# A hybrid decoder layer on one core: residual rows kept whole for the second norm, and a fixed matmul order at the mixer's end

## The chip, the cores and the metric

The kernel runs on one core of one Trainium2 chip. The metric is the device time of one execution in microseconds (us). Its engines work side by side, each through its own list of instructions in order: TensorE (PE: matmuls, and transposes as matmuls with an identity), VectorE (DVE), ScalarE (ACT) and GpSimd (POOL); SyncE (SP) starts most of the DMAs. Semaphores hold an instruction back until what it reads is there and what it overwrites is no longer needed.

## The reference

One layer on 1024 tokens of width 1024, all in float32:

```python
h = rms_norm(x, norm_mix)
xa, ga, q, f, v, g, m_a, m_b = split(h @ w_in)            # eight projections, 1024 wide each
xa  = causal_depthwise_conv(xa, conv_w, conv_b)
y_a = rg_lru(xa, ...) * gelu(ga)                          # linear recurrence along the tokens
o   = rms_norm(hgrn2_chunkwise(silu(q), k(f), log_f, v), hg_norm)   # gated attention in chunks of 32
y   = sigmoid(m_a) * y_a + sigmoid(m_b) * (o * silu(g))
x   = x + y @ w_out
h   = rms_norm(x, norm_mlp)
x   = x + square(relu(h @ w_up)) @ w_down                 # 1024 -> 4096 -> 1024
return rms_norm(x, norm_final)
```

## The kernel before

The tokens are two halves of 512 (`c` = 0, 1). The mixer walks through each half in four pairs of heads (`p` = 0 to 3): `project` multiplies the normed half by a group of weight columns (the tiles `pj_xa`, `pj_q`, `pj_f`, `pj_g`, `pj_mb`, `pj_ga`, `pj_ma`), `project_v` does so for two pairs at once (`pv`), `conv` and `rg_lru` make one branch (`xc`, then the products `pr` and `pi`, the tiles `rw`, `rr`, `ri`, `h`), `hgrn` the other (`qa`, `kb`, `qb`, `kk`, `qn` on VectorE; scores `sc` and the transposed keys `pk` on TensorE), and `gates` merges them (`on`, `gel`). Every product is split into three matmuls (`mm3`): both operands are kept as a high and a low part, made from the float32 tile by `split` (L81), a cast on ScalarE (`wH`) and a subtraction on VectorE (`wL`). So each weight tile that comes in (`raw`) costs both engines some time.

After the first half, `out_proj` multiplies the gated result by `w_out` in two passes of 512 columns (`hf` = 0, 1; four row tiles of 128 tokens each, product tiles `po`). Between the passes `first_norm` norms and transposes the second half's rows (`norm_rows`, `transposed`; rows `x`, result `xn`). `res0` loads the residual's piece into `xs` (128x512, two buffers), VectorE adds `po` to it (L739), and `done0` stores the sum to `x2d` in HBM. The rows come back whole in `early_norm` (tile `x2a`), are normed into `xna_h` and stored again, to be fetched at the mixer's end. `early_sums` adds blocks of the first weights of the MLP (tiles `qa0`, `qb0`, `qa1`, `qb1`, of the input `mlp_in`) and stores the sums. Both are written in the loop over the pairs of the second half, and their instructions lie around pair 0.

The MLP multiplies by Strassen's scheme with seven products: per group of hidden columns ("quad") the products `uX`, `uY`, `uZ` come from parts of the normed rows (`h2B11`, `h2B21`, `h2t1`, `h2n2`, `h2T3`, `h2B22`, `h2T4`) and of the weights (`wA...` for a block itself, `ws...` for sums), the first accumulating into PSUM banks from which ScalarE copies intermediate values `e`. `wA` are splits of the quad's raw tiles `q`; the raw sums `s` come back from HBM.

At the mixer's end the second half's output projection (`po`) is interleaved with the transposes of the first half's rows (`early_half`), and the last row tiles follow: `stats` squares and norms (`x2s` to `xn_h`, L888 to L892), `turned` transposes (`xT_h`, L868), `late_ops` makes the Strassen combinations. Up to there the program order of TensorE's matmuls is fixed (`pe_order[0]`, `keep_in_program_order`); from row tiles 6 and 7 (`tt` = 2, 3) on the scheduler sets it by priorities. `hidden(q, step)` issues one product and empties its bank; steps 0 and 3 of quads 0 and 1 (`uX` and `uZ`) come first, then the loop over the quads. x's rows of tiles 6 and 7 are stored to HBM as `x_6` and `x_7`.

Of the kernel before, what the change touches and what calls it, by code (L numbers as in the profile page):

```python
# [42 lines left out]
def trunk(ctx: ExitStack, tc: tile.TileContext, x, wts, mlp, pv, gains, mask_f, mask_u, out):  # L43
# [100 lines left out]

    def norm_rows(xt, xn, gain, name):
        r = const.tile([P, 1], F32, tag="rstd", name=f"rstd_{name}", bufs=4)
        keep(A.activation(xn, xt, AF.Square, scale=D**-0.5, accum_out=r))
# [1 line left out]
        keep(G.tensor_tensor(out=r, in0=r, in1=mhalf[:, 0:1], op=ALU.pow))
        keep(V.scalar_tensor_tensor(xn, xt, r[:, 0:1], gain, op0=ALU.mult, op1=ALU.mult))  # L150
# [93 lines left out]
    X_TAGS = ("g1", "g2", "on", "xc")  # L244

    def first_norm():
        dst = a2_set(a2h, "hT1")
        xts = [tile_x(f"x{4 + tt}") for tt in range(4)]
        for tt in range(4):
            nc.sync.dma_start(xts[tt], x[(4 + tt) * P : (5 + tt) * P, :])  # L250
        xns = {}

        def rows(tt):
            xns[tt] = mt("f" if tt % 2 == 0 else "tmp", f"xn1{tt}", (P, D))
            norm_rows(xts[tt], xns[tt], gain0[0], f"x1{tt}")

        rows(0)
# [639 lines left out]
    def late_rows(tt, tag, pin):  # L897
        turned(xns[tt], tag, f"h{4 + tt}", pin)

    def late_ops(o, tt):  # L900
        b11, b21, b12, b22 = parts(tt)
        if o == "t1":
            V.tensor_tensor(out=b11, in0=b11, in1=b12, op=ALU.subtract)
            op_split(b11, "t1", tt)
        elif o == "n2":
            V.tensor_tensor(out=b12, in0=b22, in1=b12, op=ALU.subtract)
            op_split(b22, "B22", tt)
            V.scalar_tensor_tensor(b22, b11, -1.0, b22, op0=ALU.mult, op1=ALU.subtract)
            op_split(b22, "n2", tt)
        elif o == "T3":  # L910
            op_split(b12, "T3", tt)
# [156 lines left out]

    e_first = ust.tile([P, 2, T], F32, tag="u2", name="e0_01", bufs=3)

    def hidden(q, step):
        bk, wo, ho = PLAN[step]
        first = (q, bk) not in bank_of
        if first:
            bank_of[q, bk] = bank(BANK[bk], f"u{bk}{q}")
# [2 lines left out]
        o, b = bank_of[q, bk], b_of[q]
        wh, wl = ops_w[q][wo]
        hh, hl = hop[ho]  # L1080
        for k in range(4):
            cols = slice(k * P, (k + 1) * P)
            mm3(o, wh[:, cols], wl[:, cols], hh[:, k, :], hl[:, k, :], first and k == 0, k == 3, not first)
# [28 lines left out]

    for q in (0, 1):
        load_quad(q)
        work[q] = quad_steps(q, (w1p, wp))
        with tc.high_priority(200):
            work[q]["a"]()
            if q == 0:
                work[0]["d"]()
            else:  # L1120
                work[1]["one"]("A12", w1p.tile([P, 2, 512], F32R, tag="w1", name="wA12_1", bufs=3))
        if q == 0:
            work[0]["sums"]()
# [206 lines left out]
```

## Time and profile before

| | |
|---|---|
| median of three runs | 1577.17 us (1572.2 to 1577.4) |
| the profiled execution | 1579.71 us, its span 1577.5 us |
| TensorE busy | 1552.7 us (98%) |
| TensorE weight loads | 1280.6 us (81%) |
| VectorE busy | 1197.6 us (76%) |
| ScalarE busy | 787.2 us (50%) |
| mean granted TensorE clock | 0.998 |

The span runs from the first to the last instruction. Rows of the waits name the waiting instruction, then what released it, then us in total, times, longest. Rows of the timeline have the start in us, the duration, engine, line, operation, tiles, shapes, and in brackets the idle time of the engine before them with what ended it; `x4` behind a row says that it stands for four such instructions. Rows of the chain have start, length and what.

### The profile page before, as it was taken

To read this page: it belongs to the slowest core of one execution; us is meant where nothing else is said; L and a number is where in the kernel's file an instruction comes from. 1 tells how busy PE (TensorE), PEld (TensorE's weight loads), DVE (VectorE), ACT (ScalarE), POOL (GpSimd) and SP (SyncE) were. 2 spreads that over 40 slices of the span, in tenths; PEclk is the share of its full clock that TensorE was granted. 3 is DMA by queue.
4 is the path that set the end of the run, shared out by engine and by line. 5 is a ranking of instruction groups with operands and counts; after the bars stand their busy time and mean duration, and the time that the engine had idled before them with its cause. 6 is when DMAs were issued, how large, how long until landed. Compare 5 with 4: busy or idle time off the path is not lost.

```text
span 1577.5 us, 22878 instructions
## 1 busy us (share of the span) xinstructions
PE 1552.7 (98%) x9002; PEld 1280.6 (81%) x9002; DVE 1197.6 (76%) x1746; ACT 787.2 (50%) x1255; POOL 76.8 (5%) x105
## 2 busy tenths in 40 slices
PE   9999999999999999999999999999999999999998
PEld 7788888888887778888888887888888878888886
DVE  5886954968763877955969788877788888888875
ACT  5644544556442644544545576776777632211115
POOL 1010000010100010000000000000000000000002
PEclk9999999999999999999999999999999999999999
DMA  6222222222245532222322454666666665666652
GB/s 231 94 81 94 91 71 93 95 74 94 88 160 200 199 110 94 95 81 83 105 80 88 146 208 151 268 252 252 248 249 252 222 265 226 246 251 254 254 211 107
DMA packets 61019, 254.88 MB, mean 162 GB/s; under 512 B 7152, under 2 KB 7280, under 8 KB 50160
## 3 DMA queue, kind: packets, MB, share of 16 engines
q1 hardware_dynamic: 59328, 248.18, 43.3%
q10 hardware_dynamic: 1584, 5.25, 1.0%
q8 instruction: 70, 1.15, 0.3%
q14 instruction: 37, 0.30, 0.1%
HBM read 189.44 MB, written 63.96 MB: 161 GB/s over the span
## 4 chain that ended last, share of the span: by engine, by line
PE 86%; DVE 9%; issue 2%; DMA 2%; ACT 1%; POOL 0%; DVEq 0%; SPq 0%; ACTq 0%; POOLq 0%
PE dX L122 10%; PE uX L122 9%; PE pj_ma L122 6%; PE pj_xa L122 6%; PE dY L122 5%; PE pj_ga L122 5%; PE pj_q L122 5%; PE pj_f L122 5%; PE uY L122 5%; PE po L122 4%; PE pj_g L122 4%; PE pj_mb L122 4%; PE pv L122 4%; PE dZ L122 2%; PE uZ L122 2%
## 5 line engine op out<-in xcount | busy, mean ns | idle before, releaser
L83 DVE TENSOR_TENSOR wL<-raw,wH 128x1024 fp32r<-128x1024 f32 x153 | 187.1, 1224 | 120.2 <-ACT wH L82 119.7
L82 ACT CAST wH<-raw 128x1024 fp32r<-128x1024 f32 x155 | 162.8, 1051 | 161.1 <-issue 34.9
L1240 DVE TENSOR_TENSOR acc<-acc,dX 128x512 f32<-128x512 f32 x128 | 86.8, 683 | 30.3 <-PE dX L122 29.7
L82 ACT CAST wA<-q 128x512 fp32r<-128x512 f32 x34 | 20.8, 621 | 131.1 <-DMA q<-mlp_in 102.6
L1240 DVE TENSOR_TENSOR acc<-acc,dY 128x512 f32<-128x512 f32 x64 | 43.4, 685 | 17.7 <-PE dY L122 15.5
L429 DVE RECIPROCAL rr<-rr 128x512 f32<-128x512 f32 x16 | 53.5, 3346 | 0.0
L1091 ACT ACTIVATE b<-b 128x512 f32<-128x512 f32 x48 | 30.2, 630 | 35.3 <-DVE b L1090 35.3
L1201 POOL TENSOR_TENSOR acc<-acc,gain 128x512 f32<-128x512 f32 x8 | 10.4, 1299 | 605.5 <-ACT junk L1198 605.2
L122 PE MATMUL uX<-h2B11H,wA 128*128 128x512 f32 x128 | 39.8, 391 | 0.0
L666 ACT ACTIVATE on<-po 128x128 f32<-128x128 f32 x64 | 16.9, 280 | 37.4 <-PE po L662 37.3
L540 POOL TENSOR_SCALAR seg<-seg 128x128 f32<-128x128 f32 (+1 forms) x16 | 19.2, 1202 | 290.5 <-DVE seg L468 290.5
L395 DVE SCALAR_TENSOR_TENSOR xc<-xp,pvt,xc 128x512 f32<-128x512 f32 x48 | 33.1, 747 | 0.0
L1092 ACT ACTIVATE b<-b 128x512 f32<-128x512 f32 x48 | 30.0, 630 | 1.1
L670 DVE TENSOR_SCALAR hssq<-hssq 128x8 f32<-128x8 f32 x8 | 1.4, 172 | 36.1 <-ACT on L666 36.1
L122 PEld LDWEIGHTS uX<-h2B11H,wA 128*128 128x128 f32 x128 | 23.9, 188 | 4.9
L122 PE MATMUL pj_ga<-hT0L,wH 128*128 128x512 f32 x64 | 26.9, 420 | 0.0
L122 PE MATMUL pj_ga<-hT1L,wH 128*128 128x512 f32 x64 | 26.5, 414 | 0.0
L122 PE MATMUL pv<-wL,hT1H 128*128 128x512 f32 x64 | 25.2, 394 | 0.8 <-DVE xs L739 0.8
L122 PE MATMUL pj_mb<-hT1L,wH 128*128 128x512 f32 x64 | 25.4, 396 | 0.0
L122 PE MATMUL pj_mb<-hT0L,wH 128*128 128x512 f32 x64 | 25.4, 396 | 0.0
L122 PE MATMUL pj_ga<-hT0H,wL 128*128 128x512 f32 x64 | 25.4, 396 | 0.0
L122 PE MATMUL uX<-h2B11L,wA 128*128 128x512 f32 x64 | 25.0, 391 | 0.3 <-ACT wA L82 0.3
(1641 smaller groups left out, 5136.7 us busy)
## 6 DMA issues: line engine op xcount, KB each, us to landing
raw<-wts_in SPq DMA_DIRECT2D x157, 512.0 KB, 3.4
q<-mlp_in SPq DMA_DIRECT2D x64, 512.0 KB, 3.6
x<-x_in SPq DMA_DIRECT2D x8, 512.0 KB, 5.9
acc<-x ACTq DMA_DIRECT2D x8, 512.0 KB, 6.2
y_out<-acc SPq DMA_DIRECT2D x16, 256.0 KB, 2.2
xs<-x_in SPq DMA_DIRECT2D x8, 256.0 KB, 4.5
x<-xs SPq DMA_DIRECT2D x8, 256.0 KB, 2.1
x2a<-x SPq DMA_DIRECT2D x4, 512.0 KB, 5.1
```

Source lines behind the costliest of these rows:

```text
L82: keep(A.copy(h, src))
L83: keep(engine.tensor_tensor(out=lo, in0=src, in1=h.bitcast(F32), op=ALU.subtract))
L122: ins = PE.matmul(o, a, b, start=begin, stop=end, **how)
L395: V.scalar_tensor_tensor(xc[:, s, :], xp[:, j : j + T], pvt[:, PV_CW + 8 * j + u : PV_CW + 8 * j + u + 1], xc[:, s, :], op0=ALU.mult, op1= ...
L429: V.reciprocal(rec, rec)
L540: G.tensor_scalar(after[:, :, 2], t4[:, :, 3], 1.0, 0.0, op0=ALU.mult, op1=ALU.add)
L666: A.activation(on[:, 4 * s + n, :], po[:, n * P : (n + 1) * P], AF.Square, accum_out=ssq[:, 4 * s + n : 4 * s + n + 1])
L670: V.tensor_scalar(ssq, ssq, 1.0 / P, EPS, op0=ALU.mult, op1=ALU.add)
L1091: A.activation(b[:, at, :], b[:, at, :], AF.Relu, scale=-1.0 if at == 2 else 1.0)
L1092: A.activation(b[:, at, :], b[:, at, :], AF.Square)
L1201: G.tensor_tensor(out=x2[t][:, cols], in0=x2[t][:, cols], in1=gain2[:, cols], op=ALU.mult)
L1240: V.tensor_tensor(out=dst, in0=dst, in1=banks[bk, pr], op=op)
```

## The change

1. Residual rows of the first half. `rows0` holds four whole rows tiles `xr0` to `xr3` (128x1024) in buffers that the mixer uses at other times (`X_TAGS`), loaded once in front of the first half's output projection. `res0` returns a slice of them; the sum is made in place, stored to `x2d`, and `early_norm` norms it from there. The loads `xs` and `x2a` are gone, and all four `early_norm` are called ahead of pair 0 of the second half.
2. The first norm of row tile 4 (`first_row(0)`) is called in `gates` of pair 3 of the first half, behind `on`, and its place in VectorE's order is fixed.
3. At the mixer's end the order of TensorE stays fixed through the products of steps 3 and 0 of quads 0 and 1 and the transposes of row tiles 6 and 7. The product (`products`) is issued apart from the emptying of its bank (`emptied`). The first weight splits and `e` get tiles in a pool that is free there (`w_first`, `e_first`), and the late combinations come in another order (`late_ops`).
4. The stores `x_6`, `x_7` go in front of the second sum load of quad 1.

```diff
-        keep(V.tensor_scalar(r, r, EPS, None, op0=ALU.add))
+        ins = keep(V.tensor_scalar(r, r, EPS, None, op0=ALU.add))
+        if pinned:
+            tc.keep_in_program_order(ins)
...
+    def first_row(tt):
+        xt = tile_x(f"x{4 + tt}")
+        nc.sync.dma_start(xt, x[(4 + tt) * P : (5 + tt) * P, :])
+        first_rows[tt] = mt("f" if tt % 2 == 0 else "tmp", f"xn1{tt}", (P, D))
+        norm_rows(xt, first_rows[tt], gain0[0], f"x1{tt}", tt == 0)
...
         on = on[0]
+        if c == 0 and p == NPAIR - 1:
+            first_row(0)
...
     def res0(tt, hf):
-        xs = xt_pool.tile([P, 512], F32, tag="xs", name=f"xs{tt}{hf}", bufs=2)
-        nc.sync.dma_start(xs, x[tt * P : (tt + 1) * P, hf * 512 : (hf + 1) * 512])
-        return xs
+        return rows0[tt][:, hf * 512 : (hf + 1) * 512]
...
     def early_norm(tt):
-        xs, xn = tile_x(f"x2a{tt}"), tile_x(f"xna_h{tt}")
-        nc.sync.dma_start(xs, x2d[tt])
-        norm_rows(xs, xn, gain1, f"h{tt}")
+        xn = tile_x(f"xna_h{tt}")
+        norm_rows(rows0[tt], xn, gain1, f"h{tt}")
...
+            for tt in range(4):
+                rows0.append(mt(X_TAGS[tt], f"xr{tt}", (P, D)))
+                nc.sync.dma_start(rows0[tt], x[tt * P : (tt + 1) * P, :])
             out_proj(0, ys, res0, done0, first_norm)
             gain1 = gain_tile(1)
+            for tt in range(4):
+                early_norm(tt)
...
-    pe_order[0] = False
-    for tt in (2, 3):
-        nc.sync.dma_start(x2d[4 + tt], x2s[tt])
-        late_rows(tt, "sc", False)
-    for o in ("t1", "n2", "T3", "T4"):
-        for tt in (2, 3):
-            late_ops(o, tt)
...
+    w_first = [a2y.tile([P, 4, 512], F32R, tag="a2", name=f"wA1{j}", bufs=4) for j in range(2)]
+    load_quad(0)
+    work[0] = quad_steps(0, (None, wp))
+    with tc.high_priority(200):
+        work[0]["one"]("A11", w_first[0][:, 0:2, :])
+        work[0]["d"]()
+    work[0]["sums"]()
+    products(0, 3)
+    nc.sync.dma_start(x2d[6], x2s[2])
+    late_rows(2, "sc", True)
+    products(0, 0)
+    load_quad(1)
...
+    products(1, 0, last_rows)
+    products(1, 3)
+    pe_order[0] = False
...
-    for q in (0, 1):
-        load_quad(q)
...
-        hidden(q, 0)
-        hidden(q, 3)
...
+    for step in (0, 3):
+        for q in (0, 1):
+            with tc.high_priority(200):
+                emptied(q, step)
```

`last_rows` is called inside `products(1, 0)` and, behind the second of its four groups, stores row tile 7 and transposes it.

On VectorE, in pair 3 of the first half, ahead of `kb` in the `hgrn` chain, the kernel before has

```order
L83 TENSOR_TENSOR wL_3486<-raw_3483,wH_3485 128x1024
L468 TENSOR_TENSOR seg_3375<-seg_3375 128x16
L148 TENSOR_SCALAR rstd_x_4079<-rstd_x_4079 128x1
L468 TENSOR_TENSOR seg_3375<-seg_3375 128x8
L150 SCALAR_TENSOR_TENSOR xn_4078<-x_4070,rstd_x_4079,gain_143 128x1024
L468 TENSOR_TENSOR kb_3374<-kb_3374,seg_3375 128x128x6
L468 TENSOR_TENSOR dd_3373<-sc_03_3531,mf 128x256
```

and the changed kernel, at the same place,

```order
L692 TENSOR_TENSOR g_3446<-g_3446,pj_g_1_3385 128x512
L84 TENSOR_TENSOR wL_3486<-raw_3483,wH_3485 128x1024
L469 TENSOR_TENSOR seg_3375<-seg_3375 128x16
L469 TENSOR_TENSOR seg_3375<-seg_3375 128x8
L469 TENSOR_TENSOR kb_3374<-kb_3374,seg_3375 128x128x6
L469 TENSOR_TENSOR dd_3373<-sc_03_3531,mf 128x256
```

so `rstd_x` and `xn`, the norm of row tile 4, have left the chain.

On VectorE, from the convolution of pair 0 of the second half (`xc`) to `q`, the kernel before has the sums of the first quad in between (L767 to L770):

```order
L385 COPY xp_5351<-xcar 128x3
L767 TENSOR_TENSOR qb_6135<-qa_6134,qb_6135 128x512
L83 TENSOR_TENSOR wL_4558<-raw_4555,wH_4557 128x1024
L83 TENSOR_TENSOR xcL_4520<-xc_4504,xcH_4519 128x1024
L385 COPY xp_5358<-xcar 128x3
L768 TENSOR_TENSOR qa_6134<-qa_6134 128x512
L769 TENSOR_TENSOR qa_6134<-qb_6135,qa_6134 128x512
L770 TENSOR_TENSOR qb_6135<-qa_6134,qb_6135 128x512
L449 TENSOR_TENSOR q_4585<-sq_4586,pj_q_0_4523 128x256x2
```

In the changed kernel the last norm and both quads' sums stand ahead of the convolution:

```order
L153 SCALAR_TENSOR_TENSOR xna_h_4313<-xr_3940,rstd_h_4314,gain_4290 128x1024
L84 TENSOR_TENSOR wL_4392<-raw_4389,wH_4391 128x1024
L84 TENSOR_TENSOR wL_4422<-raw_4419,wH_4421 128x1024
L769 TENSOR_TENSOR qb_6128<-qa_6127,qb_6128 128x512
L770 TENSOR_TENSOR qa_6127<-qa_6127 128x512
L771 TENSOR_TENSOR qa_6127<-qb_6128,qa_6127 128x512
L772 TENSOR_TENSOR qb_6128<-qa_6127,qb_6128 128x512
L84 TENSOR_TENSOR wL_4458<-raw_4455,wH_4457 128x1024
L84 TENSOR_TENSOR wL_4488<-raw_4485,wH_4487 128x1024
L769 TENSOR_TENSOR qb_6140<-qa_6139,qb_6140 128x512
L770 TENSOR_TENSOR qa_6139<-qa_6139 128x512
```

Four rows later follows the first `xc`; the second quad's sums, and the norm `xna_h` that stood ahead of `kk` in pair 0, have left the recurrence and the `hgrn` chain.

On TensorE at the mixer's end, behind the last `po`, the kernel before has (`uX_8577` is quad 0's, and row tile 7's transposes lie in quad 1's `uX` in the same way)

```order
L122 MATMUL uZ_8592<-h2B21H,wA120L 128x512
L122 MATMUL uZ_8592<-h2B21L,wA120H 128x512
L122 MATMUL uX_8577<-h2B11L,wA_8566 128x512
L868 MATMUL xT_h_0_8441<-ident,xn_h_8250 128x128 x4
L868 MATMUL xT_h_1_8447<-ident,xn_h_8250 128x128 x4
L122 MATMUL uX_8577<-h2B11H,wA_8566 128x512 x2
L122 MATMUL uX_8577<-h2B11L,wA_8566 128x512
```

with four `uZ` matmuls ahead of this `uX` and eight behind it; the changed kernel has all twelve `uZ` first:

```order
L123 MATMUL uZ_8440<-h2B21L,wA120H 128x512
L123 MATMUL uZ_8440<-h2B21H,wA120H 128x512
L123 MATMUL uZ_8440<-h2B21H,wA120L 128x512
L872 MATMUL xT_h_0_8454<-ident,xn_h_8234 128x128 x4
L872 MATMUL xT_h_1_8460<-ident,xn_h_8234 128x128 x4
L123 MATMUL uX_8466<-h2B11L,wA_8424 128x512
L123 MATMUL uX_8466<-h2B11H,wA_8424 128x512 x2
```

Row tile 6's transposes thus moved behind eight more matmuls, and nothing behind them may pass.

More of the change, by code (lines that the diff above doesn't have):

```diff
@@ L79, in keep @@
             tc.keep_in_program_order(ins)
+        return ins
     def split(src, h, lo, engine=V):
@@ L142, in gain_tile, with norm_rows @@
         return g
-    def norm_rows(xt, xn, gain, name):
+    def norm_rows(xt, xn, gain, name, pinned=False):
         r = const.tile([P, 1], F32, tag="rstd", name=f"rstd_{name}", bufs=4)
         keep(A.activation(xn, xt, AF.Square, scale=D**-0.5, accum_out=r))
-        keep(V.tensor_scalar(r, r, EPS, None, op0=ALU.add))
+        ins = keep(V.tensor_scalar(r, r, EPS, None, op0=ALU.add))
+        if pinned:
+            tc.keep_in_program_order(ins)
         keep(G.tensor_tensor(out=r, in0=r, in1=mhalf[:, 0:1], op=ALU.pow))
@@ L244, in trunk @@
     X_TAGS = ("g1", "g2", "on", "xc")
+    first_rows = {}
+    def first_row(tt):
[3 more added lines that the diff above has]
+        norm_rows(xt, first_rows[tt], gain0[0], f"x1{tt}", tt == 0)
     def first_norm():
         dst = a2_set(a2h, "hT1")
[L248 to L257, printed above, removed]
         for tt in range(4):
             if tt < 3:
-                rows(tt + 1)
-            transposed(xns[tt], dst, tt, f"x1{tt}")
+                first_row(tt + 1)
+            transposed(first_rows[tt], dst, tt, f"x1{tt}")
         hT.append(dst)
@@ L742, in out_proj @@
                 between()
+    rows0 = []
     def res0(tt, hf):
-        xs = xt_pool.tile([P, 512], F32, tag="xs", name=f"xs{tt}{hf}", bufs=2)
-        nc.sync.dma_start(xs, x[tt * P : (tt + 1) * P, hf * 512 : (hf + 1) * 512])
-        return xs
+        return rows0[tt][:, hf * 512 : (hf + 1) * 512]
     def done0(tt, hf, xs):
@@ L783, in trunk @@
             if c == 1 and p == 2:
-                early_norm(2)
                 early_sums(0)
@@ L789, in trunk @@
             px = project(c, f"xa{c}{p}")
-            if c == 1 and p != 2:
-                early_norm(p)
             if c == 0 and p == 0:
@@ L898, in late_rows @@
         turned(xns[tt], tag, f"h{4 + tt}", pin)
+    n2_of = {}
     def late_ops(o, tt):
@@ L905, in late_ops @@
         elif o == "n2":
+            n2_of[tt] = b22 if tt < 2 else x2s[tt][:, 0:512]
+            V.scalar_tensor_tensor(n2_of[tt], b11, -1.0, b22, op0=ALU.mult, op1=ALU.subtract)
+            op_split(n2_of[tt], "n2", tt)
+        elif o == "T3":
             V.tensor_tensor(out=b12, in0=b22, in1=b12, op=ALU.subtract)
+            op_split(b12, "T3", tt)
+        elif o == "B22":
             op_split(b22, "B22", tt)
[L908 to L911, printed above, removed]
         else:
-            V.scalar_tensor_tensor(b21, b22, -1.0, b21, op0=ALU.mult, op1=ALU.subtract)
+            V.scalar_tensor_tensor(b21, n2_of[tt], -1.0, b21, op0=ALU.mult, op1=ALU.subtract)
             op_split(b21, "T4", tt)
@@ L975, in trunk @@
                 late_rows(i - 1, "hg", True)
-                for o in ("t1", "n2", "T3"):
+                for o in ("t1", "T3", "B22", "n2"):
                     late_ops(o, i - 1)
@@ L1038, in one @@
         def one(o, t):
-            cols = slice(0, 512) if o == "A12" else slice(512, 1024)
-            split(raw_q[i][1][:, cols], t[:, 0, :], t[:, 1, :])
+            cols = slice(512, 1024) if o == "A22" else slice(0, 512)
+            split(raw_q[i][0 if o == "A11" else 1][:, cols], t[:, 0, :], t[:, 1, :])
             ops[o] = (t[:, 0, :], t[:, 1, :])
@@ L1050, in quad_steps, with products, last_rows @@
         }
+    work, b_of, bank_of, e_of = {}, {}, {}, {}
+    def products(q, step, inside=lambda k: None):
+        bk, wo, ho = PLAN[step]
+        first = (q, bk) not in bank_of
+        if first:
+            bank_of[q, bk] = bank(BANK[bk], f"u{bk}{q}")
+        o = bank_of[q, bk]
+        wh, wl = ops_w[q][wo]
+        hh, hl = hop[ho]
+        for k in range(4):
+            cols = slice(k * P, (k + 1) * P)
+            mm3(o, wh[:, cols], wl[:, cols], hh[:, k, :], hl[:, k, :], first and k == 0, k == 3, not first)
+            inside(k)
+    w_first = [a2y.tile([P, 4, 512], F32R, tag="a2", name=f"wA1{j}", bufs=4) for j in range(2)]
[10 more added lines that the diff above has]
+    load_quad(1)
+    work[1] = quad_steps(1, (None, wp))
+    with tc.high_priority(200):
+        work[1]["one"]("A11", w_first[0][:, 2:4, :])
+        work[1]["one"]("A12", w_first[1][:, 0:2, :])
+    def last_rows(k):
+        if k == 1:
+            nc.sync.dma_start(x2d[7], x2s[3])
+            late_rows(3, "sc", True)
+    products(1, 0, last_rows)
+    products(1, 3)
+    pe_order[0] = False
+    e_first = a2y.tile([P, 4, T], F32, tag="a2", name="e0_01", bufs=4)
+    for o in ("t1", "n2", "T3", "B22", "T4"):
+        for tt in (2, 3):
+            late_ops(o, tt)
+        if o == "t1":
+            work[0]["b"]()
+        elif o == "n2":
+            work[0]["c"]()
+    close_n2()
+    close_y()
+    w1p, close_w1 = opened("w1")
     ust, close_ust = opened("ust")
@@ L1061, in trunk @@
     u_ops = {}
-    work, b_of, bank_of, e_of = {}, {}, {}, {}
     def u_tile(pool, q, g, many):
@@ L1067, in u_tile, with emptied @@
         return t
-    e_first = ust.tile([P, 2, T], F32, tag="u2", name="e0_01", bufs=3)
     def hidden(q, step):
[L1072 to L1075, printed above, removed]
+        products(q, step)
+        emptied(q, step)
+    def emptied(q, step):
         if q not in b_of:
             b_of[q] = up.tile([P, 4, T], F32, tag="b", name=f"b{q}", bufs=2)
[L1078 to L1083, printed above, removed]
+        o, b = bank_of[q, PLAN[step][0]], b_of[q]
         if step < 3:
@@ L1111, in hidden_ops @@
         made(U_GROUPS[3], b[:, 2:4, :])
-    for q in (0, 1):
-        load_quad(q)
[L1115 to L1123, printed above, removed]
-        hidden(q, 0)
-        hidden(q, 3)
-        if q == 0:
-            work[0]["b"]()
-            work[0]["c"]()
+    for step in (0, 3):
+        for q in (0, 1):
+            with tc.high_priority(200):
+                emptied(q, step)
     work[1]["one"]("A22", w1p.tile([P, 2, 512], F32R, tag="w1", name="wA22_1", bufs=3))
```

3 lines of the change are left out of this document (removed).

## The prediction

> **What bounds the kernel.** I read the page's busy line first, then the waits of TensorE, then the chain that ended last in order of time, and last the timeline of the engines around the waits.
>
> ```profile
> PE 1552.7 (98%) x9002; PEld 1280.6 (81%) x9002; DVE 1197.6 (76%) x1746; ACT 787.2 (50%) x1255; POOL 76.8 (5%) x105
> xs<-x_in SPq DMA_DIRECT2D x8, 256.0 KB, 4.5
> x2a<-x SPq DMA_DIRECT2D x4, 512.0 KB, 5.1
> q<-mlp_in SPq DMA_DIRECT2D x64, 512.0 KB, 3.6
> ```
>
> TensorE is busy 1552.7 of 1577.5 us. The change removes no product, so all that it can gain lies in the 24.8 us in which TensorE stands idle, and in the refilling behind each stop. The three DMA rows are loads, with the time from issue to landing.
>
> ```profile
> PE uX L122 <- ACT e L1087: 3.1, 4, 1.7
> PE pk L643 <- DVE kk L468: 1.5, 1, 1.5
> PE sc L476 <- DVE qn L468: 1.5, 2, 1.0
> PE sc L476 <- DVE qa L468: 1.5, 1, 1.5
> PE pr L122 <- DVE q L449: 1.1, 1, 1.1
> PE xT_h L868 <- DVE xn_h L892: 0.8, 2, 0.5
> PE pv L122 <- DVE xs L739: 0.8, 1, 0.8
> ```
>
> Each row is what TensorE waited for: us in total, how often, the longest. These seven, 10.3 us, stand in three places that the change touches: pair 3 of the first half (`sc<-qn`), the first half's output projection and pair 0 of the second half (`pv`, `pr`, `sc<-qa`, `pk`), and the mixer's end (`xT_h`, `uX<-e`). An idle time understates its price, since the first matmul after it is slower, so I price the places by their lengths. The chain gives the starts of stages (start, length, what):
>
> ```profile
> 340.00 10.90 PE pj_xa L122 x48
> ...
> 434.10 21.78 PE po L122 x96
> ...
> 484.15 4.74 DMA xs<-x_in
> 489.76 15.04 PE pv L122 x65
> 504.80 10.88 PE pj_xa L122 x48
> ...
> 601.23 10.90 PE pj_xa L122 x48
> ...
> 693.32 21.77 PE pv L122 x96
> ...
> 899.25 8.18 PE po L122 x36
> ...
> 996.26 2.72 PE uY L122 x12
> ```
>
> A pair without these waits lasts 693.32 - 601.23 = 92.09 us (pair 1 of the second half). Pair 3 of the first half lasts 434.10 - 340.00 = 94.10, 2.0 more; pair 0 of the second half 601.23 - 504.80 = 96.43, 4.3 more. A value projection `pv` of 96 matmuls lasts 21.77; that of pair 0 starts at 481.64 (row below) and ends at 504.80, 23.16, so 1.4 more. From the mixer's last output projection (899.25) to the first `uY` that follows quads 0 and 1's hidden products (996.26) it is 97.01 us. In that stretch I count 192 `po` and 15 products of 12 matmuls, 372 at 10.88/48 = 0.2267 us, 84.3 us, and eight row tiles' transposes at some 0.87, 7.0 us, together 91.3; it loses 5.7. So 2.0 + 1.4 + 4.3 + 5.7 = 13.4 us is what the change can reach at most.
>
> ```profile
> 481.64 0.39 PE L122 MATMUL pv<-wL,hT1H 128*128 128x512 f32 x1
> 528.80 0.47 PE L122 MATMUL pr<-xcL,wH 128*128 128x512 f32 x1 [1.11 <-DVE q L449]
> 564.13 0.87 PE L476 MATMUL sc<-qa,kb 128*32 128x48 f32 x62 [1.51 <-DVE qa L468]
> 579.59 0.84 PE L643 MATMUL pk<-ident,kk 128*128 128x128 f32 x6 [1.53 <-DVE kk L468]
> ...
> 950.15 0.87 PE L868 MATMUL xT_h<-ident,xn_h 128*128 128x128 f32 x6 [0.29 <-DVE xn_h L892]
> 956.34 0.85 PE L868 MATMUL xT_h<-ident,xn_h 128*128 128x128 f32 x6 [0.53 <-DVE xn_h L892]
> 967.56 0.50 PE L122 MATMUL uX<-h2n2L,ws10H 128*128 128x512 f32 x1 [1.73 <-ACT e L1087]
> 972.20 0.50 PE L122 MATMUL uX<-h2T3L,ws30H 128*128 128x512 f32 x1 [0.72 <-ACT e L1087]
> ```
>
> **Pair 3 of the first half.** The first norm of row tile 4 moves off the hgrn chain of VectorE, behind `on`. VectorE's rows show what it costs there, and what the other moved pieces cost:
>
> ```profile
> 399.07 1.29 DVE L150 SCALAR_TENSOR_TENSOR xn<-x,rstd_x,gain 128x1024 f32<-128x1024 f32 x1 [0.53 <-POOL rstd_x L149]
> 489.01 0.69 DVE L739 TENSOR_TENSOR xs<-po,xs 128x512 f32<-128x512 f32 x1 [2.68 <-DMA xs<-x_in]
> 522.97 0.69 DVE L767 TENSOR_TENSOR qb<-qa,qb 128x512 f32<-128x512 f32 x1 [1.04 <-DMA qb<-mlp_in]
> 527.36 0.69 DVE L770 TENSOR_TENSOR qb<-qa,qb 128x512 f32<-128x512 f32 x1
> 527.97 0.68 DVE L449 TENSOR_TENSOR q<-sq,pj_q 128x512 f32<-128x512 f32 x1
> 576.35 1.28 DVE L150 SCALAR_TENSOR_TENSOR xna_h<-x2a,rstd_h,gain 128x1024 f32<-128x1024 f32 x1 [0.73 <-POOL rstd_h L149]
> 948.81 1.28 DVE L892 SCALAR_TENSOR_TENSOR xn_h<-x2s,ssq_h,gain 128x1024 f32<-128x1024 f32 x1 [0.66 <-POOL ssq_h L891]
> 954.91 1.29 DVE L892 SCALAR_TENSOR_TENSOR xn_h<-x2s,ssq_h,gain 128x1024 f32<-128x1024 f32 x1 [0.43 <-POOL ssq_h L891]
> ```
>
> 1.29 us of work and 0.53 of waiting for POOL, 1.8, stand ahead of `kb`, `qb`, `kk` and `qn`; the two waits for `qn` are 1.5 and the stage loses 2.0. With 1.8 us gone the chain is in time, and 0.2 is taken back at worst. The row is needed later, by the transposes between the halves of the first output projection, a whole gating stage and 96 matmuls on; I keep 0.3 against a wait there. Gain 1.7, bounds 0 (the wait moves) and 2.0.
>
> **The whole residual rows.** Eight loads `xs` into two buffers go, and four loads `x2a` of what was just stored. The `xs` add at 489.01 waited 2.68 us for a load (484.15, 4.74 us in the chain) that could start only when an earlier add and store had freed its buffer, and it held the PSUM bank which `pv` needed. In the changed kernel the rows are in SBUF from the start, four loads of 512 KB during the first half's projection, and the adds come at the pace of VectorE (0.69 each). Nothing is behind a DMA any more. The bank is free in time, gain 1.2, between the wait's 0.8 and the stage's 1.4.
>
> **Early norms and sums.** The norms of row tiles 0 to 3 (1.28 each, 5.1 us) and eight sums (0.69 each, 5.5 us) go ahead of pair 0's convolution. VectorE has room there:
>
> ```profile
> 480.00:500.00 20.00, 19.21 (x84) 15.37 (x84) 7.49 (x9) 5.25 (x6) 0.54 (x1) 1.00 0.67 235
> 500.00:520.00 20.00, 20.00 (x90) 16.57 (x89) 9.76 (x12) 9.60 (x15) 1.08 (x2) 1.00 0.57 195
> 540.00:560.00 20.00, 20.00 (x90) 16.55 (x89) 20.00 (x26) 12.83 (x17) 0.00 (x0) 1.00 0.54 178
> ```
>
> The third busy time is VectorE's: 7.49 and 9.76 of 20 us before the convolution, 20.00 in the window that ends at the `qa` stop. Three of the norms had been there already, so 1.28 + 5.5 = 6.8 us come into windows that were idle for 22.75. What leaves the full windows is one norm (1.28 + 0.73 wait, right ahead of the `pk` stop), eight sums of 0.69, and the 1.04 wait: 8.6 us against three stops of 4.2 us. The sums between 525.92 and 528 us delayed `q` and with it `pr`; the chain ahead of `qa` loses four more. I place the changed order by hand: adds done by 483 us, norms by 494, their stores and the loads of the sums behind them on SP (3.6 to 5.1 us each by the page's rows, the sums' loads asked for when the last norm has been stored) give the second pair of sums at 513 to 516 us, `wL` at 517, where the convolution of before starts at 517.8. So it is 0 to 0.5 late, against a slack of some 3 us before `pr` stops. I take 4.1 of 4.3. Bounds: 0, where the sums' loads are so late that the convolution hangs on them (rival 2), and 4.3. The DMA share of 0.67 at 480 to 500 us falls with twelve loads less and rises with the quads' loads; the cover is gone if a load then takes 8 us and not 4.
>
> **The mixer's end.** TensorE now takes all of `uZ` of quad 0 (12 matmuls), the transposes of row tile 6, `uX` of quads 0 and 1 with tile 7's transposes in the middle, then `uZ` of quad 1. `e` is copied from `uX` well before `n2` and `T3` products need the bank, which removes 1.73 + 0.72. New is that nothing can pass tile 6's transposes. Its norm row starts at 948.81 and ends near 950.1 in the kernel before; in the changed order three weight casts of two quads stand ahead of the second square on ScalarE, as this row's:
>
> ```profile
> 963.44 0.62 ACT L82 CAST wA<-q 128x512 fp32r<-128x512 f32 x1 [1.84 <-DMA q<-mlp_in]
> ```
>
> At 0.6 each that makes `xn_h` ready about 951.8, while the 12 `uZ` end at 950.7: one stop of 1.1. Tile 7's row is ready near 954.3 and reached at 956.7. `t1` is ready at 961.5 and reached at 961.7, so there I keep 0.2. The loss falls from 5.7 to 1.3, gain 4.4. Bounds: below nothing (rival 3) and 5.7. The stores of tiles 6 and 7 go between the sum loads on SP instead of behind the next quad's second load, and nothing on TensorE waits for them.
>
> At 950.15 the trace shows TensorE stopped for 0.29 us at tile 6's transposes with eleven `uX` matmuls behind them. [...]
>
> **The sum.** 1.7 + 1.2 + 4.1 + 4.4 = 11.4 us. The profiled execution took 1579.71 (span 1577.5), so 1568.3 on its scale; it stands 2.5 above the median 1577.17, which gives 1565.8, say 1566.
>
> **Rivals.**
> 1. Only the first half's part comes. For it: the mixer's end was tight on ScalarE and VectorE, not on TensorE alone, and two of my margins there are 0.2 us; each stop removed may return at `xT_h`, `t1` or `n2`. Against it: 2.8 us of waits for `e` are a matter of order alone. Gain 7.0, time 1570.
> 2. The early sums are late. VectorE takes its rows in order, so the convolution stands behind eight sums and these behind four loads; at 522.97 the trace shows such a wait of 1.04. If the second pair lands 3 us later than I placed it, each further us is one of TensorE. With 4 us lost the gain is 7.3, time 1570; against it, the loads have 10 us between the adds and the need.
> 3. Slower: the fixed order at the mixer's end. The second square of tile 6 stands behind casts that wait for loads of the second quad (1.84 in the row above). Whatever these loads are late by, TensorE stands, for no product may go ahead. From 4.4 us late the end gains nothing, from 11.4 the kernel is slower, from 19.3 by over 0.5%. Against it: a load takes 3.6 and is asked for 10 us ahead. At 20 us late it would be 1586.
> 4. It doesn't do what it says: the waits give way to others at the same places, since VectorE is full from 540 us on. Time 1577.
>
> **How the numbers follow.** Forecast 0.62, rival 1 0.12, rival 2 0.15, rival 3 0.05, rival 4 0.06. 0.5% is 7.9 us, about what a measurement of this kernel tells from no change: faster means under 1569.3. The forecast lies there in nine parts of ten, rivals 1 and 2 (1570) in four of ten: 0.56 + 0.11 = 0.67. Slower is most of rival 3, 0.04; the rest, 0.29, is no change. The range goes from 1561 (all 13.4 us and a run 2 us quick) to 1574: it holds the forecast and rivals 1 and 2, with the three runs' own spread of 5 us, and leaves out the last two.
>
> **What would show it.** Right: no row `pv<-xs`, no wait of a microsecond for `q`, `qa`, `kk` or `qn`; pair 0 of the second half about 92.3 us, pair 3 of the first 92.4; no `xs` or `x2a` loads; one `xT_h` wait near 1.1 and no `uX<-e` above 0.3 at the mixer's end, whose stretch lasts near 92.6. Wrong: VectorE idle on `qb<-mlp_in` around 505 to 520 us with `pr` late, or TensorE idle at tile 6's transposes for more than 4 us.

## The result and the profile after

The changed kernel takes 1568.65 us (median of six runs, 1566.74 to 1570.19), the kernel before 1577.33 in the same runs: ratio 0.9943, 95% interval 0.9932 to 0.9955, 8.7 us. In a later set of five runs, told of below, it was 1565.98 against 1577.96, ratio 0.9923 (0.9911 to 0.9935), 12.0 us. By the medians both are faster by more than 0.5%; the first set's interval reaches to 0.45%. Forecast were 1566 and 11.4 us. One execution in all, of the kernel `best` below, took 8945 us and is not compared.

The page of the changed kernel, busy times and the new loads:

```profile
PE 1548.2 (99%) x9002; PEld 1279.6 (82%) x9002; DVE 1198.3 (77%) x1746; ACT 787.5 (50%) x1255; POOL 76.9 (5%) x105
xr<-x_in SPq DMA_DIRECT2D x4, 512.0 KB, 3.8
```

The waits of TensorE in the changed kernel (us in total, times, longest):

```profile
PE xT_h L872 <- DVE ssq_h L894: 1.9, 1, 1.9
PE dZ L123 <- DVE wA1230L L84: 1.7, 1, 1.7
PE sc L477 <- issue: 1.5, 1, 1.5
PE gain_ps L293 <- DVE g0diag L292: 1.1, 1, 1.1
PE warm L282 <- DVE ones L129: 1.0, 1, 1.0
PE dX L123 <- DMA u8n<-u8n: 1.0, 1, 1.0
PE pi L123 <- DVE q L450: 0.5, 1, 0.5
```

Of the seven rows shown before, six have no counterpart (`uX<-e`, `pk`, `sc<-qn`, `sc<-qa`, `pr`, `pv`). The seventh, `xT_h`, has grown from two short waits (0.8 together) to one of 1.9. The rest lies in places that the change doesn't touch.

Where the time went is read from the first matmul of each stage. TensorE's timeline of the changed kernel, and behind it the starts in the kernel before that were not shown:

```profile
336.06 0.48 PE L123 MATMUL pj_xa<-hT0L,wH 128*128 128x512 f32 x1
428.32 0.48 PE L123 MATMUL po<-wL,y0H 128*128 128x512 f32 x1
476.31 0.39 PE L123 MATMUL pv<-wL,hT1H 128*128 128x512 f32 x1
498.07 0.39 PE L123 MATMUL pj_xa<-hT1L,wH 128*128 128x512 f32 x1
590.03 0.47 PE L123 MATMUL pj_xa<-hT1L,wH 128*128 128x512 f32 x1
887.99 0.47 PE L123 MATMUL po<-wL,y1H 128*128 128x512 f32 x1
982.40 0.39 PE L123 MATMUL uY<-h2t1L,ws12H 128*128 128x512 f32 x1
```

```profile
339.75 0.48 PE L122 MATMUL pj_xa<-hT0L,wH 128*128 128x512 f32 x1
433.85 0.48 PE L122 MATMUL po<-wL,y0H 128*128 128x512 f32 x1
504.64 0.39 PE L122 MATMUL pj_xa<-hT1L,wH 128*128 128x512 f32 x1
600.99 0.48 PE L122 MATMUL pj_xa<-hT1L,wH 128*128 128x512 f32 x1
899.00 0.47 PE L122 MATMUL po<-wL,y1H 128*128 128x512 f32 x1
996.10 0.39 PE L122 MATMUL uY<-h2t1L,ws12H 128*128 128x512 f32 x1
```

| stage (us) | before | after | gain | forecast |
|---|---|---|---|---|
| up to pair 3 of the first half | 339.75 | 336.06 | 3.7 | 0 |
| pair 3 of the first half | 94.10 | 92.26 | 1.8 | 1.7 with the next row |
| output projection of the first half | 47.79 | 47.99 | -0.2 | |
| pv of pair 0, second half | 23.00 | 21.76 | 1.2 | 1.2 |
| pair 0, second half | 96.35 | 91.96 | 4.4 | 4.1 |
| pairs 1 to 3 | 298.01 | 297.96 | 0.0 | 0 |
| mixer's end, quads 0 and 1's first products | 97.10 | 94.41 | 2.7 | 4.4 |
| the rest of the span | 581.4 | 582.6 | -1.2 | 0 |

The first and the last row lie where the change touches nothing; they are taken up below, with the granted clock. The rows between add up to 10.0 us (with the unrounded starts).

### The profile page after: what moved, and what is told of

The parts are those of the page before. It is cut to its first block, busy times and chain, and to the rows that moved or that the text cites. A ratio compares the mean times of both kernels' runs of the same rounds, so it can differ in the third digit from the quotient of the medians.

```text
span 1565.0 us, 22869 instructions
## 1 busy us (share of the span) xinstructions
PE 1548.2 (99%) x9002; PEld 1279.6 (82%) x9002; DVE 1198.3 (77%) x1746; ACT 787.5 (50%) x1255; POOL 76.9 (5%) x105
## 3 DMA queue, kind: packets, MB, share of 16 engines
q8 instruction: 70, 1.15, 0.3%
## 5 line engine op out<-in xcount | busy, mean ns | idle before, releaser
L667 ACT ACTIVATE on<-po 128x128 f32<-128x128 f32 x64 | 16.9, 280 | 36.5 <-PE po L663 36.4
L84 DVE TENSOR_TENSOR wA<-q,wA 128x512 fp32r<-128x512 f32 x34 | 23.3, 687 | 3.5 <-ACT wA L83 3.5
L1269 DVE TENSOR_TENSOR acc<-acc,dZ 128x512 f32<-128x512 f32 x32 | 21.9, 684 | 4.6 <-PE dZ L123 4.5
L123 PE MATMUL po<-wL,y0H 128*128 128x512 f32 x64 | 25.3, 395 | 0.0
```

The lines of the kernel that those rows point to most:

```text
L84: keep(engine.tensor_tensor(out=lo, in0=src, in1=h.bitcast(F32), op=ALU.subtract))
L123: ins = PE.matmul(o, a, b, start=begin, stop=end, **how)
L667: A.activation(on[:, 4 * s + n, :], po[:, n * P : (n + 1) * P], AF.Square, accum_out=ssq[:, 4 * s + n : 4 * s + n + 1])
L1269: V.tensor_tensor(out=dst, in0=dst, in1=banks[bk, pr], op=op)
```

## The experiments

Each is the changed kernel with one edit, or one part of the change alone. "Stretch" is the row of the mixer's end in the table, from the first `po` of the second half to the first `uY` of quad 2; stages were read from each kernel's own profile as above.

**The two parts apart.** `first_half` has parts 1 and 2 of the change and the mixer's end of before; `mixer_end` has parts 3 and 4 alone:

```text
 first_half:   res0, early_norm, first_row as changed; late_ops to the loop over the quads as before
 mixer_end:    res0, early_norm, first_norm as before; late_ops to the loop over the quads as changed
```

> Residual rows, early norms and the first norm of row tile 4 as in the changed kernel; the mixer's end as before. Theory (the gains are local and add): pair 3 of the first half 92.3 us, pv of pair 0 21.8, pair 0 of the second half 92.0 (before 94.1, 23.2, 96.4); from the mixer's last projection to the first uY of quad 2 97.1 as before; 7.3 us off, about 1570. Rival (half of the measured gain is a chance of the start and of the clock): the stages shorten, but the time falls by less than 5 us.

> Only the mixer's end as in the changed kernel. Theory: the stretch from the mixer's last projection to the first uY of quad 2 is 94.4 us instead of 97.1, with one stop of 2.1 us (start to start) at row tile 6's transposes; pair 0 of the second half stays 96.4; 2.7 us off, about 1574.6. Rival: the MLP behind it gives 1.4 us back because its order changed, and about 1576 is left.

`first_half` took 1571.21 us against 1578.39 (ratio 0.9960, 0.9946 to 0.9973), 7.2 us off. Stages: pair 3 92.28, pv 21.76, pair 0 91.96, stretch 97.51. Its waits still have the mixer's end of before:

```profile
PE uX L123 <- ACT e L1091: 3.2, 3, 1.7
...
PE xT_h L872 <- DVE xn_h L896: 0.8, 2, 0.5
```

`mixer_end` took 1573.55 (0.9974, 0.9962 to 0.9986), 4.8 by the medians and 2.2 to 6.0 by the interval. Its stretch is 93.68, its pair 3 94.11, its pair 0 96.68. The gains are local: each part shortens its own stages and no other. They add, within what the times can tell. The rival of `first_half`, under 5 us, does not fit its stages, which add up to 7.2; the interval of the times alone, 4.3 to 8.5 us, would just leave room for it. `mixer_end`'s, 1.4 us handed back by the MLP because of its new order, is taken up under the clock.

**Pair 3 of the first half.** `row_back`:

```diff
-        if c == 0 and p == NPAIR - 1:
-            first_row(0)
...
     def first_norm():
+        first_row(0)
```

> The changed kernel with the first norm of row tile 4 back at its old place, called at the head of the first norm and not pinned. Theory (1.8 us of VectorE work ahead of kb): the waits sc<-qn return with 1.5 us and pair 3 of the first half lasts 94.1 us instead of 92.3; the output projection behind it 47.8 instead of 48.0. Rival (another piece of the change freed that stage): it stays at 92.3.

One run, 1568.14 us. Its wait is back to the tenth, and pair 3 lasts 94.08 us (the place in VectorE's order is not fixed either):

```profile
PE sc L478 <- DVE qn L470: 1.5, 2, 1.0
```

So the 1.8 us of that stage belong to the one norm row of 1.29 us with its 0.53 of waiting. The output projection behind it lasts 48.02 us here, not the expected 47.8: the 0.2 us that it loses in the changed kernel do not come from the moved row.

**Pair 0 of the second half.** `norm_old` keeps the whole rows for the residual sum alone; the norms read them back from HBM and are called where they were called before (the code of the early sums is the same in all three kernels):

```diff
     def early_norm(tt):
-        xn = tile_x(f"xna_h{tt}")
-        norm_rows(rows0[tt], xn, gain1, f"h{tt}")
+        xs, xn = tile_x(f"x2a{tt}"), tile_x(f"xna_h{tt}")
+        nc.sync.dma_start(xs, x2d[tt])
+        norm_rows(xs, xn, gain1, f"h{tt}")
```

`sums_in_chain` keeps the early norms and puts the sums back into the chain, by fixing VectorE's order at the convolution, `q` and `f` with the sums in between:

```diff
+            if c == 1 and p == 0:
+                early_sums(0)
             q1 = q_of(c, p, qp)
...
     V.tensor_scalar(f, f, omlb[...], lb[...], op0=ALU.mult, op1=ALU.add)   # f_of
+            if c == 1 and p == 0 and s == 0:
+                early_sums(1)
```

> The changed kernel with the rows kept whole for the residual sum alone: the norms read them back from HBM and stand where they stood before, and so do the early sums. Theory (two separate causes): pv of pair 0 is 21.8 us (no add waits for a load), pair 0 is 96 to 96.6 with all three stops. Rival (the reload and the late residual loads were the cause of both): pair 0 falls to 94 or less with the residual loads gone.

> The changed kernel with the eight early sums put back into pair 0 of the second half: quad 0's four ahead of q, quad 1's four between the recurrence and f. The four norms stay early. Theory (the sums delayed q and qa): the stops at pr and sc<-qa come back at 1 to 1.7 us each, the one at pk does not, and pair 0 is 94.5 to 95.5 us (changed kernel 92.0, before 96.4). Rival (the norm ahead of kk and the loads made the stops): pair 0 stays at 92 to 92.5.

`norm_old` took 1572.89 us, pv 21.76 and pair 0 98.80. The three stops are back, the one at `pr` twice as long as before (2.1 for 1.1). TensorE's timeline:

```profile
524.46 0.47 PE L123 MATMUL pr<-xcL,wH 128*128 128x512 f32 x1 [2.12 <-DVE q L450]
561.22 0.88 PE L477 MATMUL sc<-qa,kb 128*32 128x48 f32 x63 [1.32 <-DVE qa L469]
576.68 0.85 PE L644 MATMUL pk<-ident,kk 128*128 128x128 f32 x6 [1.53 <-DVE kk L469]
```

The cause of the pv wait is thus apart from that of the three stops. Whole rows for the residual sum alone end the first (21.76), and do nothing for the others. Pair 0 is even 2.4 us worse than before, and the trace shows why. In the middle of the convolution VectorE waited 2.31 us for a load of the sums (1.04 before), so the stop at `pr` is 1.0 longer; and behind this stop the granted clock was 0.50 for 3.4 us, which is some 1.6 more, estimated from what the same drop costs at `dZ` (below). VectorE's row, and the windows view behind the stop (length, then the busy times of PE, PEld, DVE, ACT and POOL, then the granted clock, the DMA's busy share and GB/s):

```profile
515.44 0.69 DVE L770 TENSOR_TENSOR qb<-qa,qb 128x512 f32<-128x512 f32 x1 [2.31 <-DMA qb<-mlp_in]
```

```profile
521.85:525.26 3.41, 1.29 (x7) 0.76 (x6) 3.41 (x6) 2.41 (x4) 0.00 (x0) 1.00 0.80 287
525.26:528.68 3.42, 3.42 (x10) 2.64 (x9) 0.78 (x2) 0.69 (x1) 0.00 (x0) 0.50 0.79 266
```

`sums_in_chain` took 1572.09 us, pair 0 96.82. The theory had 94.5 to 95.5 with stops at `pr` and `qa`; only the one at `qa` came. In this trace no sum waits for its load, and the first `q` starts 22.4 us into the stage (521.72), where it was 23.3 before. The rival, 92 to 92.5, is far off. The two others are waits for which the trace shows no releaser:

```profile
559.39 0.88 PE L485 MATMUL sc<-qa,kb 128*32 128x48 f32 x63 [1.22 <-DVE qa L477]
563.01 0.39 PE L123 MATMUL pj_mb<-hT1H,wH 128*128 128x512 f32 x1 [0.92 <-issue]
573.55 0.19 PE L485 MATMUL sc<-qn,kk 128*32 128x32 f32 x1 [1.86 <-issue]
```

So the eight sums in the full chain, with VectorE's order fixed around them, cost all of the 4.9 us; how much the fixing itself has in it was not run apart. By which waits is not what I had written. What holds TensorE at 573.55 stays open: VectorE had written `qn` by 569.8 us, and `sc<-issue` in pair 1 of the first half (1.0 to 1.9 us in most of these kernels) has no releaser either.

**The mixer's end.** The stop at tile 6's transposes was to be 1.1 and is 1.9. ScalarE's and VectorE's timelines in the changed kernel show what stands ahead of it (`L892` is the square, `L896` the norm row):

```profile
938.21 0.62 ACT L83 CAST wA<-q 128x512 fp32r<-128x512 f32 x1 [0.78 <-DMA q<-mlp_in]
938.73 0.63 ACT L892 ACTIVATE xn_h<-x2s 128x512 f32<-128x512 f32 x1
...
940.35 1.28 DVE L896 SCALAR_TENSOR_TENSOR xn_h<-x2s,ssq_h,gain 128x1024 f32<-128x1024 f32 x1
...
941.78 1.06 PE L872 MATMUL xT_h<-ident,xn_h 128*128 128x128 f32 x8 [1.93 <-DVE ssq_h L894]
```

The cast of quad 1's A12 weights waits 0.78 us for its load, and the square behind it, whose input was ready, waits too. `cast_late` moves that cast; `unpinned` lets the scheduler set TensorE's order again from `uZ` on:

```diff
 cast_late:
-        work[1]["one"]("A12", w_first[1][:, 0:2, :])
...
     products(1, 0, last_rows)
+    work[1]["one"]("A12", w_first[1][:, 0:2, :])
 unpinned:
+    pe_order[0] = False
     products(0, 3)
...
-    late_rows(2, "sc", True)
+    late_rows(2, "sc", False)
```

> The changed kernel with the split of quad 1's A12 weights asked for behind quad 1's uX, so that its cast stands behind row tile 6's second square on ScalarE. Theory: that cast waits 0.78 us for its load and runs 0.52 ahead of the square, so the stop at the transposes falls from 2.1 to 0.8 us and the stretch from 94.4 to 93.1; 1.3 us under the changed kernel, about 1567.4. Rival: VectorE's adds and POOL's power set the stop, which stays at 2 us, and the time at 1568.7.

> The changed kernel without the fixed order of TensorE from quad 0's uZ on: row tile 6's transposes then come three uX matmuls later. Theory (whatever is ready goes into the stop): three matmuls of 0.227 us fill it, the stop falls from 2.1 to 1.4 us, and the stretch to 93.7; time 0.7 under the changed kernel, 1568. Rival (the fixed order brings the gain): waits for e come back as before, 1 to 2 us, the stretch is 95 to 97 and the time 1570 to 1571.

`cast_late`: 1566.44 us (0.9932, 0.9918 to 0.9946), stretch 92.93; its row of the transposes:

```profile
940.31 1.06 PE L872 MATMUL xT_h<-ident,xn_h 128*128 128x128 f32 x8 [0.57 <-ACT xn_h L892]
```

The stop falls by 1.36 us, as the theory had it. `unpinned`: 1568.43 us (0.9941, 0.9929 to 0.9953), stretch 93.87, the stop 1.2 us; no wait for `e` returned. So the fixed order is not what ended the 2.8 us of waits for `e`. By the stretch it costs 0.3 (`after_same`, below) to 0.5, since three matmuls are kept out of the stop. In times the two orders are alike.

Tile 6's row was read in six profiles with this code there. Without a wait for that load (`mixer_end`, `norm_old`) the stop was 1.19 and 1.18 us, close to the forecast 1.1; with load waits of 0.51 (`after_same`, below), 0.66, 0.78 and 0.80 it was 1.66, 1.80, 1.93 and 1.94. That is some 1.15 us plus the wait for the load, each time.

**The price of the fixed order.** `slow_2` does tile 6's second square three times:

```diff
+        for _ in range(2 if tt == 2 and not first else 0):
+            A.activation(xn[:, cols], x2s[tt][:, cols], AF.Square, scale=D**-0.5)
         A.activation(xn[:, cols], x2s[tt][:, cols], AF.Square, scale=D**-0.5, accum_out=mine)
```

> The changed kernel with row tile 6's second square done three times, which puts it and what the scheduler lets past it some 2.7 us later on ScalarE (two squares of 0.53, a weight cast of 1.0, tile 7's square). Theory (nothing may pass in the fixed order, each us is one of TensorE): the stop at tile 6's transposes is 4.8 us instead of 2.1, the stretch to quad 2's first uY 97.1 instead of 94.4. Rival (work behind catches up, as its operands are then ready): the stretch grows by 1.5 or less. If the granted clock falls after the longer stop, the stretch is over 98.

One run, 1572.35 us; the stretch is 101.77, 7.4 more and not 2.7:

```profile
945.95 1.94 PE L872 MATMUL xT_h<-ident,xn_h 128*128 128x128 f32 x8 [6.44 <-DVE xn_h L898]
```

The stop grew by 4.5, because on VectorE the norm row of tile 7 (941.54 in that trace) now stood ahead of tile 6's (944.51). Nothing caught up behind it. Some 2.1 us came on top, an estimate from the 4.50 us behind the stop at a granted clock of 0.52 (windows view), and some 0.9 in two later waits of `uX` (0.5 and 0.4):

```profile
945.90:950.40 4.50, 4.45 (x15) 3.91 (x16) 2.55 (x5) 3.03 (x6) 0.00 (x0) 0.52 0.51 190
950.40:955.00 4.60, 4.60 (x26) 3.88 (x25) 3.83 (x7) 2.88 (x6) 0.00 (x0) 1.00 0.00 1
```

So rival 3's mechanism is real, and its price was above one for one here: 7.4 us of stretch for 4.5 of stop.

**The order of the combinations.** `late_old` makes tile 6's and 7's combinations in another order, with the splits of quad 0's sum weights behind them all:

```diff
-    for o in ("t1", "n2", "T3", "B22", "T4"):
+    for o in ("t1", "T3", "B22", "n2", "T4"):
         for tt in (2, 3):
             late_ops(o, tt)
-        if o == "t1":
-            work[0]["b"]()
-        elif o == "n2":
-            work[0]["c"]()
+    work[0]["b"]()
+    work[0]["c"]()
```

> The changed kernel with the Strassen combinations of row tiles 6 and 7 in another order (t1, T3, B22, n2, T4, and quad 0's sum weights split behind them all instead of in between). Theory (the order of the combinations is what the products behind t1 wait for): uX with n2 waits 1 to 2 us, the stretch is 95.5 to 96.5 us instead of 94.4. Rival (the waits for e went because the products were taken apart from their emptying): no new wait over 0.5, and the stretch stays within 0.4 of 94.4.

One run, 1567.8 us; the stretch is 94.46, the stop at the transposes 1.2, and `n2` costs one wait of 0.6:

```profile
PE xT_h L872 <- DVE ssq_h L894: 1.2, 1, 1.2
...
PE uX L123 <- DVE h2n2L L84: 0.6, 1, 0.6
```

Set against kernels with a stop of 1.2 (`mixer_end` 93.68, `norm_old` 93.65), the order is worth some 0.8 us; the quads behind take another order too, so only the stretch is compared. The theory's 1 to 2 us at `n2` did not come; the rival's "no new wait over 0.5" is missed by a little, its stretch is right. Since neither the fixed order nor this one brings the waits for `e` back, what is left is that the products are issued apart from `emptied`; this was not undone by itself.

**A kernel beyond both.** `best` is `cast_late` with tile 6's transposes behind three `uX` matmuls in the fixed order:

```diff
+    def sixth_rows(k):
+        if k == 0:
+            nc.sync.dma_start(x2d[6], x2s[2])
+            late_rows(2, "sc", True)
+
     products(0, 3)
-    nc.sync.dma_start(x2d[6], x2s[2])
-    late_rows(2, "sc", True)
-    products(0, 0)
+    products(0, 0, sixth_rows)
```

> The changed kernel with two edits at the mixer's end: the split of quad 1's A12 weights asked for behind quad 1's uX (as in cast_late), and row tile 6's transposes placed in the fixed order behind the first three uX matmuls of quad 0. Theory: the cast's 1.3 us and three matmuls of 0.227 fill the stop of 2.1, of which under 0.2 is left; the stretch from the mixer's last projection to quad 2's first uY is 92.3 us (changed kernel 94.4, cast_late 92.9), the time 0.6 under cast_late's. Rival (t1 or n2 is next in line): the stretch stays at 92.9.

It took 1565.8 us (median of five, 1566.2 with the long execution; 0.9924, 0.9908 to 0.9940). Its profile is of the long one, so the same kernel ran again as `best_look`, beside the changed kernel as `after_same`:

> The changed kernel itself, beside the next one on the same chip. Stages as in its first profile: pair 3 of the first half 92.3, pair 0 of the second 92.0, the mixer's end 94.4 us with a stop of 2.1; about 8.7 us under before, 1569. What the start (34.6 or 36.4 us to the first xa product) and the clock behind the stop at dZ give is open: theory (chance, not the change): a second profile shows another value in at least one of them.

> The kernel of best once more, for its profile. Theory: tile 6's stop is under 0.2 us, the stretch from the mixer's last projection to quad 2's first uY 92.3 us, 2.1 under the changed kernel's, and the time on the same chip 1.5 to 3 us under it. Rival (the next product in line waits instead): the stretch is 92.9 or more.

`after_same` 1565.98 us (1564.76 to 1567.41), `best_look` 1565.09 (1561.33 to 1570.55), both 0.9923 of before (0.9911 to 0.9935 and 0.9910 to 0.9935). The stop at tile 6, 0.57 in `cast_late`, is gone in `best_look`, but the stretch is 92.97, as in `cast_late`: 0.2 us came back as a wait at `uY`, and TensorE was busy for 92.79 us of the stretch, not 92.36:

```profile
PE uY L123 <- ACT e L1131: 0.2, 1, 0.2
```

The rival was right there. By the stretch `best` is 1.2 us ahead of `after_same` (94.14), as much as the moved cast brings alone; by the times the two can't be told apart, where 1.5 to 3 us were expected.

**What differs where the code is the same.** Up to pair 3 of the first half the four computing engines have the same instructions in the same order; the DMA queue's loads differ from 9.8 us on. The first xa product starts at 34.5 to 34.8 us in six profiles and at 36.3 to 36.5 in seven, the second value in `before` (36.50) and in variants of the changed kernel (`row_back` 36.36, `late_old` 36.33), the first in both profiles of the changed kernel (34.82, 34.55). The difference arises ahead of all loads that differ, in four matmuls; the first row is of `before`, the second of the changed kernel:

```profile
5.48 3.78 PE L292 MATMUL gain_ps<-g0diag,ones 128*128 128x512 f32 x4 [1.08 <-DVE g0diag L291]
5.49 1.98 PE L293 MATMUL gain_ps<-g0diag,ones 128*128 128x512 f32 x4 [1.10 <-DVE g0diag L292]
```

They take 3.75 to 3.78 us in the seven profiles and 1.98 or 1.99 in the six. The trace's records of the full clock start at 9.1 to 10.6 us in the seven, behind these matmuls, and at 3.9 to 5.0 in the six, ahead of them. So 1.7 us of the gain between the two profiles come from when the full clock was granted. The change does nothing there, but only the changed kernel was profiled twice, with the first value both times; that it is chance was not shown.

Pair 1 of the first half lasts 92.31 (`best_look`) to 96.01 (`before`). There TensorE stops for up to 1.9 us at `sc` (not at all in `best_look`), and in `before` the granted clock falls behind it to 0.50 for 3.42 us; windows view of `before`:

```profile
198.34:201.75 3.41, 1.49 (x53) 1.21 (x42) 2.31 (x5) 2.59 (x6) 0.00 (x0) 1.00 0.35 107
201.75:205.17 3.42, 3.42 (x14) 2.92 (x13) 0.81 (x3) 0.59 (x2) 1.59 (x4) 0.50 0.16 59
```

The same happens behind the wait for `dZ`, in the profile of the changed kernel (first two rows), and not in that of `late_old`, whose wait is longer (1.81 for 1.72, last two rows):

```profile
1250.88:1254.29 3.41, 1.73 (x7) 0.78 (x5) 3.41 (x6) 3.29 (x5) 0.00 (x0) 1.00 0.86 291
1254.29:1257.70 3.41, 3.37 (x8) 2.69 (x9) 3.41 (x5) 1.27 (x3) 0.00 (x0) 0.50 0.97 398
...
1251.83:1255.24 3.41, 2.58 (x11) 1.49 (x9) 3.41 (x7) 3.16 (x6) 0.00 (x0) 1.00 0.84 292
1255.24:1258.65 3.41, 2.42 (x11) 2.00 (x12) 3.41 (x5) 2.13 (x4) 0.00 (x0) 1.00 0.99 405
```

From the end of this wait it takes TensorE 12.58 to 12.64 us to get 48 matmuls on in `after`, `after_same`, `cast_late` and `unpinned` (waits of 1.59 to 1.81), and 11.01 to 11.05 in the nine other profiles (1.55 to 1.81): the drop costs 1.6 us, and the length of the wait does not tell whether it comes. With the DMA waits of `dX` in some profiles (`u8n` 1.0 in `after`, 1.5 in `mixer_end`, none in `best_look`) this makes the rest of the span 580.5 to 584.9 us. Against `mixer_end`'s rival: its MLP lost 1.3 us against `before`, but it has a DMA wait of 1.5, and `row_back`, with the same mixer's end, has 580.6 for the 581.4 of `before`.

## Why the prediction was right

- The view was right. All that the change gained lies in places where the waits named stops of TensorE. In pair 0 the length of the stage gave their price better than the idle times (4.4 us, where the three waits were 4.1); at the mixer's end it gave too much, see below.
- Pair 3 of the first half: 1.7 forecast, 1.8 less 0.2 measured, and `row_back` shows the cause of the 1.8. The 0.3 that were kept against the transposes are not what was lost: the 0.2 stay when the row is put back, and their cause is open.
- The whole rows: 1.2 forecast, 1.2 measured, and `norm_old` keeps it without the rest.
- Early norms and sums: 4.1 forecast, 4.4 measured. Rival 2 did not come, but it was near. VectorE did wait for the second pair's load ahead of the convolution, as these rows of the changed kernel show:

```profile
507.63 0.69 DVE L769 TENSOR_TENSOR qb<-qa,qb 128x512 f32<-128x512 f32 x1 [1.84 <-DMA qb<-mlp_in]
...
511.56 4.06 DVE L396 SCALAR_TENSOR_TENSOR xc<-xp,pvt,xc 128x512 f32<-128x512 f32 x6
```

  The convolution starts 13.5 us into the stage, 13.1 before: 0.4 late, inside the 0 to 0.5 of the prediction, and `pr` did not stop. `sums_in_chain` shows that the sums have to leave the chain; the argument by which stops they act was only half right.
- The mixer's end: 4.4 forecast, 2.7 measured (3.0 in `after_same`). This is the term that was mis-sized, in two places. The price of three casts ahead of the square was right (1.18 and 1.19 against 1.1, where the load was early), though two of them cast `h2T4` and only one a weight; that this one waits for its load, 0.5 to 0.8 us, was seen as rival 3 and not put into the sum. The other 0.9 us are in the length without losses, 91.3 by the prediction's count. TensorE was busy for longer than that, in `before` (first row) and in the changed kernel (second row):

```profile
899.00:996.10 97.10, 93.21 (x439) 76.14 (x438) 83.42 (x116) 67.83 (x115) 2.69 (x4) 1.00 0.57 207
887.99:982.40 94.41, 92.41 (x439) 76.23 (x438) 82.17 (x114) 68.00 (x116) 3.10 (x4) 1.00 0.58 208
```

  So `before` stood idle for 3.9 us of the 5.7 that were to be won, and of these the change took 1.9; the other 0.8 are matmuls that take less time. With nearly no idle time left, `best_look` still lasts 92.97.
- Forecast 11.4, measured 10.0 over the stages of the change, 8.7 and 12.0 by the two sets of medians. That the second comes so near the forecast is in part luck: the stages give 10.0, and when the full clock starts, and whether it falls behind a stop, shifts single executions by 1.6 to 1.7 us each, which the forecast did not have. The profiled run of before stood 2.5 above its median; pair 1 of the first half, with the fallen clock (96.01 us there, 93.5 to 94.3 in most profiles), would account for some 2 of it.
- Rivals 1 and 4 fall: both parts bring time, and what the change says it does, it does.

## What to carry to other kernels

Work that isn't due can stand in a chain that is; moving one norm and eight sums of VectorE, 6.8 us, to windows where it idles made no new stop and removed all three behind it. When an order is fixed, look at what stands ahead of the operand's producers on the other engines: here a cast that waited 0.51 to 0.80 us for a load held the square behind it, and TensorE with it, one for one (stops of 1.66 to 1.94 us, for 1.18 and 1.19 without that wait). Compare stages from one matmul to another, not medians, when the effect is under one percent: the lengths of stages repeat within 0.15 us where no stop lies in them, while executions of one kernel here spread over 2.7 to 9.2.

## What was not expected of the hardware

The granted clock fell behind single stops of about 2 us and less. It was 0.50 for 3.4 us at 1254.29 us in `after` (behind a stop of 1.72), at 201.75 in `before` (1.9) and at 525.26 in `norm_old` (2.12); behind the stop of 6.44 us in `slow_2` it was 0.52 for 4.5 us. Seven of the 13 profiles have such a drop, four of them at `dZ`. There it costs 1.6 us on top of the stop (12.6 for 11.0 us over 48 matmuls); in `slow_2` it is some 2.1 by the estimate above.

The length of the stop does not tell whether the clock falls. At `dZ` it fell behind stops of 1.59 to 1.81 us in four profiles and stayed at 1.00 behind the 1.81 of `late_old`. What decides it was not shown.
